# A two-layer encoder trunk: the weight sums' transfers get a list of their own

## The chip, the cores and the metric

The kernel runs on one core of one Trainium2 chip. The metric is device time in microseconds (us): 1640.66 us before the change, the median of three runs from 1640.5 to 1641.07. The engines are TensorE (PE, matrix products), VectorE (DVE), ScalarE (ACT), GpSimd (POOL) and SyncE (SP). SP and POOL also issue DMA transfers, each in the order in which they stand in its own instruction queue; SP's go by DMA queue q1, POOL's by q0.

## The reference

Two layers (DEPTH = 2) over 512 tokens of width 1024, all in float32. Each layer computes

```python
h = _rmsnorm(x, g_mix[l])
proj = h @ w_in[l]                 # 4 gates | conv | three attentions' q, k, v
ys = stack([y_a, y_b, y_c, y_d])   # conformer convolution, neighbourhood, dilated, windowed attention
branch = einsum('bsnc,ncd->bsnd', ys, w_branch[l])
gates = sigmoid(gate_pre + gate_b[l])
x = x + sum(gates * branch, axis=2) @ w_out[l]
x = x + _conv_ffn(_rmsnorm(x, g_ffn[l]), w_up[l], ffn_conv_w[l], ffn_conv_b[l], w_down[l])
```

The feed-forward part (FFN) goes up from 1024 to 2 x 2816, through a width-3 convolution and SwiGLU, and down again to 1024.

## The kernel before

**Products and weights.** Every float32 product is made of three matmuls (lines 273 to 275): both operands are split into a high and a low part. A unit of weights is 512 KB: `weights` (line 248) loads it into a `w_raw` tile, ACT makes `w_hi` (line 252) and DVE `w_lo` (line 254). The units stand in a fixed list, SP issues their loads in that order, and a load waits until its `w_raw` tile is free, that is until the split of an earlier unit is done. There are two `w_raw` tiles; in the FFN two more (`w_more`) are used as well for the units of the "seven" steps, below.

**A layer's stages.** Input projections and attention run interleaved; then come four gates, one after the other (`gates`, line 840), the output projection, and the FFN (`ffn`, line 1052, then `down`). A gate has eight blocks of 24 matmuls. For each block DVE takes the product out of PSUM (`t`, line 849), ACT makes the sigmoid's tanh, and after a short product with the branch's output DVE makes another `t` (line 878) and POOL adds it to the running mix (`mx`, line 879). In the last gate ACT and DVE then split the mix for the output projection (`mh`, line 883, and `ml`, line 884).

**Sums of weights.** Parts of the FFN use products on sums of weight blocks, with seven products in place of eight. The sums are made by DMA in DRAM, all issued by POOL and all behind a matmul that was last when they were written into the program (`paced`). `quarter_sums` makes `qS` for five pieces of the up-projection in 40 transfers of 512 KB. `weight_sums` (line 1133) makes `sums` for the down-projection in 24 transfers: three chunks (1024, 1024 and 768 KB of source) in eight rounds. Rounds 1 and 2 copy a block of W into s3 and s1, rounds 3 and 4 add another block of W to these, round 5 copies s3 to s2, round 6 adds to s2, round 7 copies s2 to s4 and round 8 adds to s4. Copies of s3 and s2 stand in the profile as `sums<-sums`, all else as `sums<-W`. `down` reads `sums`; nothing before it does.

**Side work.** While PE's main stream is written, `tick` (line 887) is called twice a block or unit: in the middle and at the end. Each tick advances every generator in the list `side` by one step: attention, convolution, norms, and the sums, which `slowly` spaces: 12 ticks of delay, then one tick for each quarter sum and four for each weight sum. At the end of the third gate stands

```python
for n in ORDER[:3]:
    self.gates(n)
while self.side:
    self.tick()
```

so that whatever is still in `side` is written into the program there, ahead of the last gate. By then 8 of the 24 weight sums have been written, and the other 16 follow in one run, all behind the same matmul. The output projection has no ticks. The FFN's up-projection begins with 8 ordinary blocks (`whole`), then come 35 "seven" units of 24 shorter matmuls (128x256, line 992) and then 16 ordinary blocks.

Of the kernel before, what the change touches and what calls it, by code (L numbers as in the profile page):

```python
# [218 lines left out]
class Trunk:  # L219
# [667 lines left out]
    def tick(self):  # L887

        for g in list(self.side):

            with self.tc.issue_after(self.last_mm.ins):
                r = next(g, 'end')
            if r == 'end':
                self.side.remove(g)
            if r in ('end', 'free') and g is self.head:
                self.head = None
                self.activate()
        return bool(self.side)

    def activate(self):  # L900
# [422 lines left out]
    def run(self):  # L1323
        nc, tc = self.nc, self.tc
        with ExitStack() as st:
# [36 lines left out]
            self.w_emitted = self.w_used = 0  # L1362
            self.first_hi = None
            self.w_ready, self.w_fast = [], 0
            self.side, self.waiting, self.head = [], [], None

            self.cst = self.const.tile([P, NRES], F32, name="cst", tag="cst", bufs=1)
            self.ident = self.cst[:, C_ID:C_ID + P]
# [40 lines left out]
    def layer(self, l):  # L1409
        tc = self.tc  # L1410
        last = l == L - 1
        self.Y, self.mixed, self.MH, self.glu_u = [None] * 4, [], [], []
        with tc.tile_pool(name="gate", bufs=1, reuse_waits="tile") as self.gp:
            with tc.tile_pool(name="attn", bufs=1, reuse_waits="tile") as self.ap:
                self.scratch = lambda: self.gp.tile([P, S], F32, name="raw", tag="t1", bufs=2)
                pss = self.token_major(None, self.aux) if l == 0 else self.early
                Q = self.new_Q()
                for b in range(NB):
                    self.evac_q(Q)(b, pss[b])
                with self.first():  # L1420
                    for _ in self.qk_stats(Q, 4, 4, None):
                        pass
                self.derive_params()
                V = self.new_V()
                self.tabs = [None] * 4
                self.queue(chain(self.na_biases(l, 3 if l else 5), self.qk_norm(Q, 4, 4, 0),
                                 self.attention('na', V, 1)))
                self.side.append(self.slowly(chain(self.quarter_sums(l), self.weight_sums(l))))
                Vd = self.new_V()
                self.project_v(V, Vd)  # L1430
                Q = self.project_qk()
                ready = self.beside(self.qk_stats(Q, 4, 4, 0))
                self.queue(chain(ready, self.qk_norm(Q, 4, 4, 2), self.attention('dil', Vd, 2)))
                self.glu()
                self.side.append(self.conv())
                V = self.new_V()
                Q = self.project_swa(V)
                ready = self.beside(self.qk_stats(Q, 4, 2, 2))
                self.queue(chain(ready, self.qk_norm(Q, 4, 2, 4), self.attention('swa', V, 3)))
# [4 lines that stand above are left out]
            with tc.tile_pool(name="outp", bufs=1, reuse_waits="tile") as self.op:  # L1444
                self.gates(ORDER[3])
                self.xnew = self.new_res()
                self.start_norm('g_ffn')
                for d in range(0, KT, 2):

                    cuts = (0, KT - 2, KT) if d == 0 else (0, KT)  # L1450
                    pss, ws = [self.mm(), self.mm()], []
                    for k0, k1 in zip(cuts, cuts[1:]):
                        for e in range(2):
                            if k0 == 0:
                                ws.append(self.unit())
                            hi, lo = ws[e]
                            for k in range(k0, k1):
                                s = slice(k * P, (k + 1) * P)
                                self.prod(pss[e], hi[:, s], lo[:, s], self.MH[k][0], self.MH[k][1], k == 0,
                                          k == KT - 1)  # L1460
                            if k1 == KT:
                                self.update(d + e, pss[e], self.op)
                self.xres = self.xnew
                self.broadcast_norm()
        if last:
            self.resT = self.dram.tile([S, D], F32, name="resT", tag="resT", bufs=1)
        with tc.tile_pool(name="ffn", bufs=1, reuse_waits="tile") as self.fp:
            self.scratch = lambda: self.fp.tile([P, S], F32, name="raw", tag="cy0", bufs=2)
            F = self.ffn(l, last)
            if last:  # L1470
                self.down(F, True)
                return
            self.load_prm(l + 1)
            self.xnew = self.new_res()
            self.sq_tag = "fth"
            self.start_norm('g_mix')
            self.down(F, False)
            self.finish_norm(5, 8, 4)

            self.early = self.token_major(None, self.aux)  # L1480
            self.xres = self.xnew
            self.sq_tag = "sq"
# [45 lines left out]
```

## Time and profile before

| | |
|---|---|
| median of three runs | 1640.66 us |
| the profiled execution's own time | 1639.18 us |
| its span, first to last instruction | 1637.4 us |
| mean granted TensorE clock | 0.971 |
| PE busy | 1541.0 us (94%) |
| DVE, ACT, POOL busy | 1251.0, 895.8, 205.4 us |
| `sums<-W`, 24 of 1024 KB and 12 of 768 KB | 12.3 and 16.8 us to landing (median) |
| `sums<-sums`, 8 and 4 | 17.0 and 11.9 us |

The times in a chain or timeline row are start and length in us from the span's start. A row of windows has the busy time of PE, PEld (weight load), DVE, ACT and POOL with the count of instructions, then the granted clock, the mean busy share of the 16 DMA engines, and GB/s. A "wait" names who waited, on whom, us in all, how often, and the longest.

### The profile page before, as it was taken

How to read it: one execution, taken by the hardware profiler on the slowest of the kernel's cores; microseconds unless marked ns; L12 is line 12 of the kernel's file. 1: busy time of each engine (PE TensorE's matmuls, PEld its weight loads, DVE VectorE, ACT ScalarE, POOL GpSimd, SP SyncE). 2: the span in 40 equal slices, each digit the busy share in tenths (PEclk: the TensorE clock that was granted, in tenths of full speed). 3: DMA queues.
4: the chain of work that ended last, by engine and by line, in shares of the span. 5: the costliest groups of instructions: out<-in, count | busy, mean ns of one | idle time of the engine just before them, and what ended most of it. 6: DMA issues, size and time to landing. Idle time of an engine off the chain costs nothing.

```text
span 1637.4 us, 21918 instructions
## 1 busy us (share of the span) xinstructions
PE 1541.0 (94%) x7842; PEld 1311.0 (80%) x7842; DVE 1251.0 (76%) x2114; ACT 895.8 (55%) x1504; POOL 205.4 (13%) x308
## 2 busy tenths in 40 slices
PE   9999999990999999999999999999809999999999
PEld 7888888870788998888888888888708889988887
DVE  6699988740669999986576899887306699999964
ACT  6778777320446665464457686763204556655643
POOL 0044122122110000000002231122221000000000
PEclk9999999995999999999999999999959999999999
DMA  7788764599673554356567988645996747753565
GB/s 233 226 232 229 205 173 142 157 204 236 155 265 103 180 185 136 96 182 202 184 183 222 249 224 197 171 158 157 199 231 170 264 119 209 208 157 93 173 221 166
DMA packets 124797, 306.84 MB, mean 187 GB/s; under 512 B 28176, under 2 KB 30096, under 8 KB 124688
## 3 DMA queue, kind: packets, MB, share of 16 engines
q1 hardware_dynamic: 93712, 212.10, 40.8%
q0 software_dynamic: 30688, 92.81, 25.3%
q8 instruction: 62, 1.02, 0.2%
q10 hardware_dynamic: 288, 0.52, 0.1%
q14 instruction: 47, 0.39, 0.1%
HBM read 287.56 MB, written 100.67 MB: 237 GB/s over the span
## 4 chain that ended last, share of the span: by engine, by line
PE 83%; DMA 6%; DVE 4%; ACT 3%; issue 3%; POOL 2%; SPq 0%; POOLq 0%; ACTq 0%; DVEq 0%
PE mm L273 15%; PE mm L274 15%; PE mm L275 15%; PE aux L992 11%; DMA sums<-sums 4%; PE aux L1225 2%; PE aux L1223 2%; PE aux L1224 2%; PE mm L502 2%; PE mm L504 2%; PE mm L503 2%; PE mm L1224 2%; PE mm L1225 2%; PE mm L1223 2%; PE mm L992 2%
## 5 line engine op out<-in xcount | busy, mean ns | idle before, releaser
L252 ACT ACTIVATE w_hi<-w_raw 128x1024 fp32r<-128x1024 f32 (+1 forms) x335 | 350.9, 1047 | 382.1 <-PE mm L274 127.1
L254 DVE TENSOR_TENSOR w_lo<-w_raw,w_hi 128x1024 fp32r<-128x1024 f32 (+1 forms) x335 | 407.3, 1217 | 94.5 <-ACT w_hi L252 92.3
L273 PE MATMUL mm<-xh,w_hi 128*128 128x512 f32 x960 | 377.3, 393 | 89.5 <-DVE t L849 89.5
L275 PE MATMUL mm<-xh,w_lo 128*128 128x512 f32 x960 | 376.1, 392 | 0.0
L274 PE MATMUL mm<-xl,w_hi 128*128 128x512 f32 x960 | 375.9, 392 | 0.0
L273 PEld LDWEIGHTS mm<-xh,w_hi 128*128 128x128 f32 x960 | 181.5, 189 | 126.9 <-ACT w_hi L252 90.3
L275 PEld LDWEIGHTS mm<-xh,w_lo 128*128 128x128 f32 x960 | 181.1, 189 | 39.7 <-DVE w_lo L254 1.1
L274 PEld LDWEIGHTS mm<-xl,w_hi 128*128 128x128 f32 x960 | 181.6, 189 | 36.4
L992 PE MATMUL aux<-form,w_hi 128*128 128x256 f32 x640 | 116.1, 283 | 0.0
L884 DVE SCALAR_TENSOR_TENSOR ml<-mx,mh 128x512 fp32r<-128x512 f32 x16 | 11.0, 690 | 124.0 <-ACT mh L883 123.8
L992 PEld LDWEIGHTS aux<-form,w_hi 128*128 128x128 f32 x640 | 100.0, 192 | 0.2
L440 DVE SCALAR_TENSOR_TENSOR cv<-cv,prm 128x512 f32<-128x512 f32 x120 | 93.7, 780 | 0.7
L992 PE MATMUL aux<-form,w_lo 128*128 128x256 f32 x320 | 90.6, 283 | 0.0
L879 POOL TENSOR_TENSOR mx<-mx,t 128x512 f32<-128x512 f32 x44 | 65.2, 1487 | 156.7 <-DVE t L878 141.8
L883 ACT ACTIVATE mh<-mx 128x512 fp32r<-128x512 f32 x16 | 10.0, 627 | 135.4 <-POOL mx L879 130.9
L502 PE MATMUL mm<-w_hi,xh 128*128 128x512 f32 x192 | 76.4, 398 | 0.4 <-DVE V L630 0.4
L1033 ACT ACTIVATE cy<-U,prm 128x512 f32<-128x512 f32 x88 | 68.7, 807 | 12.7 <-DVE U L1070 7.6
L503 PE MATMUL mm<-w_lo,xh 128*128 128x512 f32 x192 | 75.0, 390 | 0.0
L504 PE MATMUL mm<-w_hi,xl 128*128 128x512 f32 x192 | 74.8, 390 | 0.0
L1110 POOL DMA_DIRECT2D qS<-W x60 | 43.6, 727 | 217.9 <-PE aux L780 107.0
L767 ACT ACTIVATE e<-e,rl 128x256 f32<-128x256 f32 (+2 forms) x96 | 57.3, 597 | 22.2 <-DVE rl L766 21.9
L849 DVE TENSOR_TENSOR t<-mm,RB 128x512 f32<-128x512 f32 x64 | 43.8, 684 | 30.3 <-PE mm L275 30.0
(339 smaller groups left out, 3297.8 us busy)
## 6 DMA issues: line engine op xcount, KB each, us to landing
w_raw<-W SPq DMA_DIRECT2D x213, 512.0 KB, 3.8
qS<-W POOLq DMA_DIRECT2D x60, 512.0 KB, 6.5
sums<-W POOLq DMA_DIRECT2D x24, 1024.0 KB, 12.3
w_raw<-qS SPq DMA_DIRECT2D x40, 512.0 KB, 3.7
w_raw<-W SPq DMA_DIRECT2D x66, 256.0 KB, 3.9
w_raw<-sums SPq DMA_DIRECT2D x44, 256.0 KB, 3.8
w_raw<-sums SPq DMA_DIRECT2D x22, 512.0 KB, 4.6
qS<-qS POOLq DMA_DIRECT2D x20, 512.0 KB, 4.9
```

The lines of the kernel that those rows point to most:

```text
L252: w = nc.scalar.activation(hi[:, s], raw[:, s], AF.Copy)
L254: nc.vector.tensor_tensor(lo[:, s], raw[:, s], hi[:, s].bitcast(F32), ALU.subtract)
L273: mm(ps, lhsT=wh, rhs=xh, start=start, stop=False)
L274: mm(ps, lhsT=wh, rhs=xl, start=False, stop=False)
L275: self.last_mm = mm(ps, lhsT=wl, rhs=xh, start=False, stop=stop)
L440: self.after_mm(v.scalar_tensor_tensor(acc, u[:, t:t + S], w(t), acc, ALU.mult, ALU.add))
L502: mm(pss[b], lhsT=self.Xh[k][:, t], rhs=hi[:, s], start=k == 0, stop=False)
L503: mm(pss[b], lhsT=self.Xh[k][:, t], rhs=lo[:, s], start=False, stop=False)
L504: self.last_mm = mm(pss[b], lhsT=self.Xl[k][:, t], rhs=hi[:, s], start=False, stop=k == KT - 1)
L992: self.last_mm = nc.tensor.matmul(o, lhsT=w[:, s], rhs=x, start=start and not (e or j or i), stop=j == 3 and i == 2, skip_group_check=True)
L1033: nc.scalar.activation(y, u[:, 1:513], AF.Identity, scale=w(1), bias=self.par('ffn_conv_b', c))
L1223: mm(ps, lhsT=x[0], rhs=w[0][:, cols], start=start, stop=False, skip_group_check=again)
```

## The change

The weight sums' generator (quarter sums and weight sums together) is no longer put into `side`. It goes into a new list `slow`, which `tick` advances after `side`, by one step a tick as before. The loop `while self.side` no longer sees it, so the generator is not emptied ahead of the last gate; the ticks of the last gate and of the FFN carry on with it. The transfers themselves and their pacing on the last matmul stay.

```diff
@@ tick
             if r in ('end', 'free') and g is self.head:
                 self.head = None
                 self.activate()
+        for g in list(self.slow):
+            if next(g, 'end') == 'end':
+                self.slow.remove(g)
         return bool(self.side)
@@ run
-            self.side, self.waiting, self.head = [], [], None
+            self.side, self.slow, self.waiting, self.head = [], [], [], None
@@ layer
-                self.side.append(self.slowly(chain(self.quarter_sums(l), self.weight_sums(l))))
+                self.slow.append(self.slowly(chain(self.quarter_sums(l), self.weight_sums(l))))
```

The order of PE's and of SP's instructions stays as it was. What moves stands on POOL. First place: POOL, first layer, from the end of the third gate into the last one, before. `mx<-mx,t` is the adding of a block to the mix; t_3908 and t_3957 are the last gate's first two. The sixteen rows from `sums_2683` on are the run that is emptied; the first three and the last two are shown.

```order
L879 TENSOR_TENSOR mx<-mx,t_3756 128x512
L1133 DMA sums_2682<-W 512x512
L879 TENSOR_TENSOR mx<-mx,t_3766 128x512
L1133 DMA sums_2683<-W 384x512
L1133 DMA sums_2681<-W 512x512
L1133 DMA sums_2682<-W 512x512
...
L1133 DMA sums_2682<-W 512x512
L1133 DMA sums_2683<-W 384x512
L879 TENSOR_TENSOR mx<-mx,t_3908 128x512
L879 TENSOR_TENSOR mx<-mx,t_3957 128x512
```

The same place after the change (the three chunks are now called sums_2705, 2706 and 2707, and t_3893 is the last gate's first add):

```order
L879 TENSOR_TENSOR mx<-mx,t_3766 128x512
L1136 DMA sums_2706<-W 512x512
L1136 DMA sums_2707<-W 384x512
L879 TENSOR_TENSOR mx<-mx,t_3893 128x512
L879 TENSOR_TENSOR mx<-mx,t_3942 128x512
L1136 DMA sums_2705<-W 512x512
L879 TENSOR_TENSOR mx<-mx,t_3992 128x512
L879 TENSOR_TENSOR mx<-mx,t_4041 128x512
L1136 DMA sums_2706<-W 512x512
L879 TENSOR_TENSOR mx<-mx,t_4097 128x512
L879 TENSOR_TENSOR mx<-mx,t_4146 128x512
L1136 DMA sums_2707<-W 384x512
```

Of the sixteen, four now stand between the last gate's six adds on POOL, and no add stands behind more than two of them. Second place: POOL at the start of the FFN, after the change. `xf<-res` loads the FFN's input for the sums of its own blocks; before the change nothing of `sums` stood there.

```order
L946 DMA xf<-res_4187 128x512
L946 DMA xf<-res_4188 128x512
L1136 DMA sums_2705<-sums_2705 512x512
L1136 DMA sums_2706<-sums_2706 512x512
L1136 DMA sums_2707<-sums_2707 384x512
L1136 DMA sums_2705<-W 512x512
L1136 DMA sums_2706<-W 512x512
L1136 DMA sums_2707<-W 384x512
```

These rounds 5 and 6 and, behind them, rounds 7 and 8 (six more rows) are now written by the ticks of the up-projection, four ticks apart; the second layer is moved in the same way.

## Prediction

> **What bounds the kernel now.** I began with the page's slices: PE is busy nearly everywhere, but for one empty slice in each layer.
>
> ```profile
> PE   9999999990999999999999999999809999999999
> ```
>
> The groups (busy and mean of one, then idle time before it and its releaser) and the list of waits say what ends the empty stretches:
>
> ```profile
> L273 PE MATMUL mm<-xh,w_hi 128*128 128x512 f32 x960 | 377.3, 393 | 89.5 <-DVE t L849 89.5
> L883 ACT ACTIVATE mh<-mx 128x512 fp32r<-128x512 f32 x16 | 10.0, 627 | 135.4 <-POOL mx L879 130.9
> ```
>
> ```profile
> PE mm L273 <- DVE t L849: 89.5, 2, 45.1
> PE aux L1378 <- DVE warm L1375: 1.2, 1, 1.2
> ```
>
> All of PE's idle time worth naming is one wait on `t` (line 849), twice: 45.1 us and, by difference, 44.4. ACT's `mh` in turn waits for POOL's `mx`.
>
> The chain of work shows who holds `t`. These pieces (start, length) are from the first layer's last gate:
>
> ```profile
> 334.87 0.76 POOL mx L879
> ...
> 339.69 3.00 POOL sums L1133 x3
> ...
> 356.62 20.82 DMA sums<-sums
> ...
> 380.29 14.96 DMA sums<-W
> ...
> 395.66 9.81 DMA sums<-sums
> ...
> 408.16 0.95 POOL sums L1133
> 409.11 1.29 POOL mx L879
> 410.42 0.64 ACT mh L883
> ...
> 411.69 0.69 DVE t L849
> ...
> 412.52 0.76 PE mm L273
> ...
> 416.92 0.36 PE mm L273
> 417.28 0.23 PE mm L274
> ```
>
> From 339.69 on POOL issues the run of 16 sums. Rounds 5 to 8 each need the round before to have landed, and POOL waits for that in its queue. The last gate's first add stands behind the run, at 409.11; ACT's `mh` waits for the add, DVE's `ml` for `mh`, and the next block's `t` stands behind `ml` on DVE. PE has run ahead as far as its PSUM banks go and then stops. The windows tell the same: while the 16 DMA engines are full, PE does 1.42 us of work in 46.
>
> ```profile
> 343.00:366.00 23.00, 23.00 (x103) 19.05 (x102) 5.05 (x6) 3.48 (x5) 2.71 (x4) 1.00 1.09 243
> 366.00:412.00 46.00, 1.42 (x7) 0.84 (x5) 0.92 (x2) 1.57 (x2) 9.39 (x11) 0.57 1.03 232
> 520.00:630.00 110.00, 110.00 (x875) 108.07 (x875) 105.02 (x140) 72.79 (x95) 0.00 (x0) 1.00 0.53 173
> 1340.00:1450.00 110.00, 110.00 (x882) 108.40 (x881) 105.83 (x138) 72.53 (x94) 0.00 (x0) 1.00 0.73 201
> ```
>
> So two things are to be weighed: the stall that goes, and what the twelve sums that now run in the FFN do to its weight loads (the last two rows, the seven stages of the two layers, where PE and DVE are both full).
>
> **What goes.** The waits: 89.5 us. Behind each, PE runs at a lower granted clock (0.57 in the stretch that holds the first). From 412.52 to 417.28 ten matmuls start, 4.76 us, where a step at full clock is 0.23 us, as at 417.28: 2.3 us, so 2.5 are lost. In the second layer thirteen start between these two pieces of the chain:
>
> ```profile
> 1227.19 0.77 PE mm L273
> ...
> 1233.14 0.24 PE mm L274
> ```
>
> That is 5.95 us in place of 13 x 0.23 = 3.0, so 3.0 are lost. Together 89.5 + 2.5 + 3.0 = 95.0 us. No other wait of PE is over 1.2 us, and PE's order is the same, so nothing on PE grows behind it.
>
> **What is late next in the last gate.** Four of the sums stand between the six adds on POOL. The third gate shows what that is like:
>
> ```profile
> 322.08 1.06 POOL L1133 DMA_DIRECT2D sums<-W  x1 [6.91 <-PE aux L478]
> 328.81 1.29 POOL L879 TENSOR_TENSOR mx<-mx,t 128x512 f32<-128x512 f32 x1 [4.36 <-DVE t L878]
> ```
>
> A sum takes POOL 1.06 us and is released by PE, and POOL then waits 4.36 us for DVE: POOL is early. Each of the four adds to what has been written many transfers before, so POOL should not wait for a landing. Cost nothing; if they held POOL, that is rival C. The stored sums are not late: twelve of them, four ticks apart, are written by the 48th of the up-projection's 118 ticks, and `down` reads them after that. The quarter sums move past one or two small POOL operations; POOL idles before them, so this costs nothing.
>
> **What the sums cost in the FFN.** Four of the twelve fall on the first eight blocks, 24 matmuls x 0.23 = 5.5 us each, where a unit is wanted only every 5.5 us: nothing. The other eight, 7424 KB (7.6 MB), fall on the seven stage, of which this is a piece of the chain:
>
> ```profile
> 540.06 17.28 PE aux L992 x144
> ```
>
> 144 matmuls, 24 a unit, in 17.28 us: a unit passes in 2.88 us, and eight sums, two units apart, are issued in 46 us. How early the loads are there shows the timeline: a split, the load that it lets go, and that load's own split, four units on (four `w_raw` tiles); below it the loads' median in that stage.
>
> ```profile
> 561.72 1.21 DVE L254 TENSOR_TENSOR w_lo<-w_raw,w_hi 128x1024 fp32r<-128x1024 f32 x1
> 562.96 0.33 SPq L248 DMA_DIRECT2D w_raw<-W  x1
> 571.71 1.06 ACT L252 ACTIVATE w_hi<-w_raw 128x1024 fp32r<-128x1024 f32 x1 [0.69 <-PE aux L992]
> ```
>
> ```profile
> w_raw<-qS SPq DMA_DIRECT2D x18, 512.0 KB, 3.4
> ```
>
> A load thus has 571.71 - 562.96 = 8.75 us; it needs 3.4 there, so 5.3 are spare. Beside sums it needs more: here a lone sum with a load (322 to 323 us), and a load in the full run (343 to 346).
>
> ```profile
> sums<-W POOLq DMA_DIRECT2D x1, 1024.0 KB, 14.5
> w_raw<-W SPq DMA_DIRECT2D x1, 512.0 KB, 8.6
> ```
>
> ```profile
> w_raw<-W SPq DMA_DIRECT2D x1, 512.0 KB, 10.0
> ```
>
> 8.6 to 10.0 us: about 1.3 more than there is, once, if loads that are under way together keep the pace. Whether they do is read from 357 to 362 us, where a pair of loads runs against two or more sums (packets, MB, share of 16 engines); below it the second layer's small stores:
>
> ```profile
> q0 software_dynamic: 263, 0.52, 55.6%
> q1 hardware_dynamic: 250, 0.96, 50.9%
> ```
>
> ```profile
> resT<-xn SPq DMA_DIRECT2D x32, 64.0 KB, 3.8
> ```
>
> q1 moved 0.96 MB in 5 us, 192 GB/s, and q0 104. The first layer's seven stage wants 173 GB/s by its window (0.524 MB in 2.88 us is 182): the loads keep pace, and only the 1.3 us for the first late one are lost; I take 1. The second layer's wants 201, since it stores the residual stream's transpose (`resT`) beside the loads. 7.6 MB at 104 GB/s last 73 us, in which q1 falls 9 GB/s x 73 us = 0.66 MB short, 1.25 units, 3.6 us of PE; I take 3, since part of the 5.3 spare us is left. Bounds: 0 (the spare time swallows it; below nothing is excluded, since PE has no idle time there to win back) and rival A's upper end. I stay near the lower end because the 357 to 362 row has both queues full, which is the state in question.
>
> Sum: 95 - 1 - 3 = 91 us. The profiled execution took 1639.18 (its span of 1637.4 and 1.8 around it) and becomes 1548.2; the median of the runs is 1.5 above it, 1640.66 - 91 = 1549.7.
>
> **Rival A: the sums take the loads' share (0.33).** By time rather than bytes: the run of sums cost
>
> ```profile
> q0 software_dynamic: 3991, 10.69, 102.8%
> ```
>
> 102.8% of 46 us for 10.69 MB, 4.42 us a MB, so eight sums are 33.6 us of all engines. Loads and stores want 0.53 and 0.73 of the engines. If each queue gets half, the sums last 67 us; the second layer falls behind by 0.23 x 67 / 0.73 = 21 us less 5 spare, 16, the first by 0.03 x 67 / 0.53 = 4, nothing after the spare time. With 1 for the first late load: 1640.66 - 95 + 17 = 1563. If the sums always go first, loads get 46 - 33.6 = 12.4 us of 46 where they want 24.4 and 33.6: behind by 12/0.53 - 5 = 17 and 21.2/0.73 - 5 = 24, together 1587. For it: 105 of 110 us busy on DVE, so a late split is not made up. Against it: the 192 GB/s. The Trainium skill ("DMA: Bandwidth & Descriptors", section "Queues, rings and completion order") says that each engine goes round its queues, a whole packet of descriptors from one before the next, whatever their size. By that rule the second layer's stores, cut small, would give a full turn to the sums for few bytes of their own, and the time would go to this rival's upper half; the first layer agrees with near one to one in the row above, 263 and 250, while no row here has small stores beside sums.
>
> **Rival B: slower than before (0.05).** If loads beside a sum land one at a time, as the lone one did, one each 8.6 us, for as long as twelve sums at 14.5 us run (174 us), a layer gets 20 units and six that were ahead; undisturbed, 26 units take 8 x 5.5 + 18 x 2.88 = 96 us. It loses 78 a layer: 1640.66 - 95 + 156 = 1702. It ends on the slower side once loads land over 5.6 us apart for all that time (47.5 us lost a layer). Against it: 0.96 MB in 5 us is one each 2.7 us.
>
> **Rival C: POOL still waits in the last gate (0.05).** If each of its four sums held POOL for one landing (8.6 to 14.5 us), half of each stall would stay: 1640.66 - 47 = 1593. Against it: the order, in which a round stands three transfers or more behind the one that it needs, and the third gate.
>
> **How the numbers follow.** The forecast, 0 to 9 us lost in the FFN, 1545 to 1555, has 0.57. The range goes from 1543 (nothing lost, and 2 for what runs differ) to 1572, which takes in rival A's equal shares; A's upper part, B and C, some 0.18 in all, lie outside. A measurement tells 0.2%, 3.3 us, from no change. Faster by more: 0.57 + 0.33 + 0.05 less a little, 0.94; slower 0.05; same 0.01.
>
> **What would show it.** Right: no wait of PE on line 849 over 2 us; POOL's adds in the last gate 6 us apart; granted clock 1.0 throughout; `sums` spread over the last gate and some 120 us of the FFN. For the forecast, PE in the two seven stages idle for under 5 us in all. Rival A would show waits of PE on `w_hi` or `w_lo` there, most in the second layer, and loads landing in over 9 us; B the same in the first layer's and in the ordinary blocks too; C POOL idle before sums of the last gate, released by DMA. A wait of `down`'s loads on `sums` would make me wrong in another way.

## The result and the profile after

The changed kernel takes 1586.76 us (median of four runs, 1583.33 to 1588.51), beside 1640.58 us for the kernel before, now the median of four runs: a ratio of 0.9673, 95% interval 0.9653 to 0.9694. It is faster by 54 us where 91 were forecast, and outside the range. The profiled execution's span is 1584.3 us, its mean granted clock 0.99.

The slices of the page after, PE and its clock: the two empty slices are gone, and weaker ones stand a little later in each layer.

```profile
PE   9999999999979999999999999999999789999998
PEclk9999999999989999999999999999999899999999
```

PE's waits after (in all, times, longest). Nothing waits on line 849 any more; what is new are 18.9 us on `U`, the first product of the FFN's up-projection, and 8.2 on `sv`, of the seven stage.

```profile
PE mm L273 <- DVE U L1073: 18.9, 2, 10.4
PE aux L995 <- ACT sv L1007: 8.2, 4, 5.7
```

PE runs the same 7842 matmuls in the same order in both kernels, so the start of each can be compared between the two traces; the difference grows or shrinks only where time is lost or won. By stages (us, minus is won):

| | first layer | second layer |
|---|---|---|
| last gate | -47.3 | -47.5 |
| output projection | +1.2 | 0.0 |
| start of the FFN | +10.8 | +12.4 |
| seven stage | +0.5 | +14.8 |

With 0.5 ahead of all this and 1.5 between the layers, the total is -53.1. So 94.8 us went, as the 95.0 of the forecast; 23 came back at a place that the forecast had at nothing, and 15 in the second layer's seven stage, where it had 3.

The last gate on POOL, first layer: two of the sums, each followed by an add that comes when DVE's `t` is there.

```profile
368.09 1.00 POOL L1136 DMA_DIRECT2D sums<-W  x1
372.01 1.29 POOL L879 TENSOR_TENSOR mx<-mx,t 128x512 f32<-128x512 f32 x1 [2.92 <-DVE t L878]
...
378.40 1.03 POOL L1136 DMA_DIRECT2D sums<-W  x1
385.05 1.29 POOL L879 TENSOR_TENSOR mx<-mx,t 128x512 f32<-128x512 f32 x1 [5.62 <-DVE t L878]
```

The windows of the last gate, of the first layer's seven stage and of the second's beginning (PE, PEld, DVE, ACT, POOL, then clock, DMA share, GB/s). PE does 45.32 of 46 us where it did 1.42, and 44.77 of 45 in the first layer's seven stage, but 24.06 of 32 in the second's, at a clock of 0.91:

```profile
366.00:412.00 46.00, 45.32 (x198) 36.67 (x197) 28.55 (x38) 19.61 (x26) 8.38 (x7) 1.00 0.70 176
...
500.00:545.00 45.00, 44.77 (x374) 44.57 (x373) 41.57 (x56) 29.64 (x39) 5.89 (x7) 1.00 1.06 323
...
1281.00:1313.00 32.00, 24.06 (x187) 23.45 (x186) 20.90 (x28) 14.28 (x18) 2.86 (x4) 0.91 1.09 289
```

**The start of the FFN.** POOL in the first layer, from the last gate's last add on:

```profile
393.21 1.30 POOL L879 TENSOR_TENSOR mx<-mx,t 128x512 f32<-128x512 f32 x1 [6.87 <-DVE t L878]
439.27 0.95 POOL L1136 DMA_DIRECT2D sums<-W  x1 [44.76 <-DVE xl L336]
...
440.02 4.30 POOL L946 DMA_DIRECT2D xf<-res  x7
451.68 0.54 POOL L946 DMA_DIRECT2D xf<-res  x1 [7.36 <-DMA sums<-W]
```

The output projection has no ticks, so the next sum (the twelfth, the last of round 4) is written by the first tick of the up-projection and paced on a matmul there. POOL comes to it at 393 and stands before it until 439.27. Behind it in POOL's queue stand the eight loads of `xf`. Before the change they went out one by one during the output projection, as each piece of the result had been stored (first and last):

```profile
450.76 0.62 POOL L943 DMA_DIRECT2D xf<-res  x1 [6.55 <-DMA res<-xn]
...
484.96 0.54 POOL L943 DMA_DIRECT2D xf<-res  x1 [4.53 <-DMA res<-xn]
```

Now they go out in a burst, behind 768 KB that must be read, added and written in the same DMA queue. The chain of work after shows what that delays:

```profile
394.51 44.74 issue
...
440.02 12.71 DMA xf<-res
452.75 1.35 ACT xf L953 x2
454.12 0.43 DVE forms L958
...
466.05 0.61 DVE U L1073
466.80 0.76 PE mm L273
```

The first `xf` lands after 12.71 us. ACT, in order, waits for it to scale it; DVE's `forms` wait for ACT and stand on DVE ahead of the last steps of the norm (lines 308 to 312), whose `RB` the first `U` needs; PE has filled its PSUM banks and stands. None of it needed `xf` so soon: it is the order on four queues that joins them.

**The second layer's seven stage.** A piece of its chain, and SP's queue there:

```profile
1286.80 18.80 DMA w_raw<-qS
...
1305.71 1.06 ACT w_hi L252
...
1309.68 0.49 ACT sv L1007
...
1310.22 4.96 PE aux L995 x24
```

```profile
1289.86 6.50 SPq L248 DMA_DIRECT2D w_raw<-W  x1
...
1298.16 4.83 SPq L248 DMA_DIRECT2D w_raw<-qS  x1
...
1311.30 0.33 SPq L248 DMA_DIRECT2D w_raw<-W  x1
```

A weight load takes 18.8 us to land, more than twice the 8.75 us that it has, and SP stands 6.50 and 4.83 us in the issue of a load that takes 0.33 otherwise. The two DMA queues (packets, MB, share), first in 27 us of the first layer (500 to 527), then of the second (1281 to 1308):

```profile
q0 software_dynamic: 1516, 3.55, 59.8%
q1 hardware_dynamic: 1266, 4.66, 45.5%
```

```profile
q0 software_dynamic: 1795, 4.56, 73.6%
q1 hardware_dynamic: 3007, 3.27, 39.7%
```

Before the change, with nothing of q0 beside it, q1 had this in the same stages (27 us, 527 to 554, and 25 us, 1340 to 1365):

```profile
q1 hardware_dynamic: 1269, 4.66, 53.7%
```

```profile
q1 hardware_dynamic: 4938, 4.70, 69.6%
```

In the first layer q1 still gets 4.66 MB, 173 GB/s, just what the stage wants: 0.5 us are lost. In the second, with the small stores in q1, its share of the engines falls from 69.6 to 39.7%, and it gets 3.27 MB, 121 GB/s, where it wants 188 to 201.

### The profile page after: what moved, and what is told of

It is laid out like the page before. It is cut to its first block, busy times and chain, and to the rows that moved or that the text cites. A ratio compares the mean times of both kernels' runs of the same rounds, so it can differ in the third digit from the quotient of the medians.

```text
span 1584.3 us, 21946 instructions
## 1 busy us (share of the span) xinstructions
PE 1546.5 (98%) x7842; PEld 1315.5 (83%) x7842; DVE 1251.0 (79%) x2114; ACT 896.5 (57%) x1504; POOL 206.0 (13%) x308
## 4 chain that ended last, share of the span: by engine, by line
PE 76%; issue 7%; DMA 7%; DVE 6%; ACT 4%; POOL 0%; ACTq 0%; POOLq 0%; DVEq 0%
PE mm L273 13%; PE mm L274 13%; PE mm L275 13%; PE aux L995 8%; DMA w_raw<-qS 3%; PE aux L1228 3%; PE aux L1227 3%; PE aux L1226 3%; PE mm L502 2%; PE mm L1228 2%; PE mm L1227 2%; PE mm L1226 2%; PE mm L504 2%; PE mm L503 2%; DMA xf<-res 2%
## 5 line engine op out<-in xcount | busy, mean ns | idle before, releaser
L273 PE MATMUL mm<-xh,w_hi 128*128 128x512 f32 x960 | 377.0, 393 | 18.9 <-DVE U L1073 18.9
L995 PE MATMUL aux<-form,w_hi 128*128 128x256 f32 x640 | 120.0, 289 | 9.6 <-ACT sv L1007 8.2
L995 PEld LDWEIGHTS aux<-form,w_hi 128*128 128x128 f32 x640 | 102.6, 197 | 10.8 <-ACT sv L1007 9.0
L1037 DVE SCALAR_TENSOR_TENSOR cy<-U,prm,cy 128x512 f32<-128x512 f32 x88 | 64.3, 748 | 1.7 <-ACT cy L1036 1.7
L1038 DVE SCALAR_TENSOR_TENSOR cy<-U,prm,cy 128x512 f32<-128x512 f32 x88 | 65.0, 746 | 0.3
```

The lines of the kernel that those rows point to most:

```text
L273: mm(ps, lhsT=wh, rhs=xh, start=start, stop=False)
L995: self.last_mm = nc.tensor.matmul(o, lhsT=w[:, s], rhs=x, start=start and not (e or j or i), stop=j == 3 and i == 2, skip_group_check=True)
```

## The experiments

All start from the changed kernel. The table has the median and, by the same comparison of matmuls with the kernel before, what each run lost at the FFN's start and in the seven stage (first / second layer).

| run | median us | FFN's start | seven stage |
|---|---|---|---|
| changed kernel | 1586.76 | 10.8 / 12.4 | 0.5 / 14.8 |
| one earlier | 1564.73 | 0.0 / 0.0 | 0.6 / 14.3 |
| small twelfth | 1574.33 | 2.0 / 7.2 | 2.2 / 16.0 |
| stores moved | 1571.20 | 9.8 / 11.2 | 0.2 / 0.0 |
| both mended | 1551.51 | 0.0 / 0.0 | 0.7 / 0.0 |
| stores in both layers | 1597.29 | 11.5 / 12.9 | 17.0 / 13.5 |
| whole stores | 1599.76 | 12.7 / 10.7 | 16.2 / 13.8 |
| stores by ACT | 1593.91 | 10.8 / 12.9 | 0.5 / 20.9 |
| bytes only | 1592.35 | 10.3 / 11.9 | 7.1 / 14.2 |
| transposes only | 1591.48 | 10.8 / 13.2 | 0.0 / 17.6 |
| bytes and transposes | 1588.02 | 10.9 / 11.4 | 7.2 / 12.1 |
| load unwaited | 1592.34 | 10.6 / 11.7 | 9.0 / 13.4 |
| pieces unwaited | 1604.89 | 11.1 / 13.0 | 21.6 / 13.5 |

Where only the first layer was touched, the second layer's stage varies from 12.1 to 17.6: what a single profile tells of that stage is good to some 3 us.

**Theories.** For the FFN's start, Q: the eight `xf` loads come late because they stand behind the twelfth sum, on POOL and in its DMA queue. Against it R1: the sum's place doesn't count; and Q1, in which its bytes don't. For the second layer's seven stage, T: it is the stores of the stream's transpose beside the sums; R2: the stores don't count.

**One earlier.** At the third gate's end the sums' list is advanced by one tick more. PE's and SP's order stays, and DVE's and ACT's but for one step a layer, which goes back to its place before the change; each sum is paced on a matmul one tick earlier, so that the twelfth is written in the last gate and stands ahead of its last add on POOL, not in the FFN.

```diff
 while self.side:
     self.tick()
+    for g in self.slow:
+        next(g)
```

> Theory Q: in each layer the twelfth weight sum is released only by the first block of the FFN, stands on POOL ahead of the eight xf loads, and its packets lie ahead of theirs in q0; the loads land 10 us late, ACT and DVE wait for them in order, and PE loses 10.8 and 12.4 us at the start of the two FFNs. Here all sums are released one tick earlier, so the twelfth is released by the last gate; nothing else moves on any engine. Q expects xf loads one by one during the output projection, no PE wait on U at the FFN's start, and 23 us less than the changed kernel: 1564. Rival R1 (the FFN's start is slow because sums run beside its loads at all, whatever the order): the sums still run there, so most of the loss stays, 1578 to 1587.

1564.73 us, ratio 0.954 (0.9524 to 0.9556). POOL, the twelfth sum, and the first and last `xf`:

```profile
389.69 0.94 POOL L1136 DMA_DIRECT2D sums<-W  x1
...
405.61 0.62 POOL L946 DMA_DIRECT2D xf<-res  x1 [4.79 <-DMA res<-xn]
...
439.81 0.54 POOL L946 DMA_DIRECT2D xf<-res  x1 [4.86 <-DMA res<-xn]
```

The sum goes out 50 us earlier, the loads go one by one again, and PE's wait on `U` is gone in both layers. Q holds, R1 falls; the second layer's seven stage isn't touched by it.

**Small twelfth.** The twelfth sum stays where it is, but moves 16 of its 384 rows; the other 368 are left out.

```diff
-                add(part(t, d), part(src, s), accum_op=ALU.add)
+                n = slice(0, 16) if d == s1 and t is items[2][1] else slice(None)
+                add(part(t, d)[n], part(src, s)[n], accum_op=ALU.add)
```

> The twelfth sum moves 16 of its 384 rows (352 rows and 16 of the third chunk's s1 are thus not added), with its place on POOL and its release unchanged. Q as stated, with both halves needed (late issue, and 12 us of packets ahead in q0): the eight loads still go out in one burst after 439 us, but the first lands within 5 us in place of 13, so of the 23 us at the two FFN starts 15 to 21 go: 1566 to 1572. Q1, the late issue alone is the cost: less than 6 us go, 1581 or more.

1574.33 us (1571.68 to 1576.99), between the two, 2 above Q's range. PE's waits and the burst on POOL:

```profile
PE mm L273 <- DVE U L1073: 5.9, 2, 4.2
```

```profile
438.14 3.97 POOL L946 DMA_DIRECT2D xf<-res  x7
```

The wait falls from 18.9 to 5.9 us, and the loss at the two FFN starts from 23.2 to 9.2: the bytes ahead of the loads in the queue make some 60% of it, the late burst itself the rest.

**Stores moved.** `turn_res` is called for two tiles each from unit pair 7 on, behind the sums and the seven stage, instead of for one each from pair 0; its load is pinned behind the matmul written last.

```diff
-        if self.last and i % 2 == 1 and i // 2 < KT:
-            self.turn_res(i // 2)
+        if self.last and i % 2 == 1 and i // 2 >= 7:
+            for d in (i - 15, i - 14):
+                self.turn_res(d)
...
-        nc.sync.dma_start(xr, self.xres[d])
+        self.after_mm(nc.sync.dma_start(xr, self.xres[d]))
```

> The second layer's stores of the transposed residual stream (64 KB, in pieces of 128 bytes), with their loads and DVE transposes, are moved behind the seven stage. Theory T: the loss of 14.7 us in the second layer's seven stage comes from these small stores sharing a queue with the weight loads and the engines with the sums. T expects a loss there of 1 or less, as in the first layer (0.5): 1573. Rival R2 (the second layer's seven stage is late because it began with less lead after a longer stall at the FFN's start, 12.4 against 10.8): the loss stays, 1585 to 1588.

1571.2 us, ratio 0.9583 (0.9568 to 0.9597). The second layer's seven stage loses nothing; of the two waits that were new, only the one on `U` is left:

```profile
PE mm L273 <- DVE U L1074: 16.8, 2, 8.6
```

**Stores in both layers.** The first layer, which lost 0.5, does the second's transposes and stores too, into a tile of its own that nobody reads.

```diff
-        if self.last and i % 2 == 1 and i // 2 < KT:
+        if i % 2 == 1 and i // 2 < KT:
...
-        if last:
-            self.resT = self.dram.tile([S, D], F32, name="resT", tag="resT", bufs=1)
+        self.resT = self.dram.tile([S, D], F32, name="resT", tag="resT", bufs=2)
```

> The first layer also does the loads, transposes and small stores of the residual stream that the second does (into a place that nothing reads); more work, nothing left out. T expects the first layer's seven stage to lose what the second's does, 10 to 15 us in place of 0.5: 1597 to 1602. R2 expects no change there: within 4 us of 1587.

1597.29 us (1596.1 to 1598.49): the first layer's seven stage now loses 17.0, a little over T's 10 to 15. T holds from both sides. Both layers also run the same sums and units, so it is this step that sets them apart. The step is loads, transposes and stores together; which of them costs, these two runs don't tell.

**Both mended.** One earlier and stores moved together.

> Both mends at once: sums released one tick earlier, and the second layer's small stores behind its seven stage. If Q and T are two separate losses, their parts add: 1587 less 22 (the run with the earlier release) less 15.6 (the run with the stores moved), 1549; PE idle for under 5 us in both FFNs. If they are one loss counted twice (an earlier start gives the seven stage its lead back), more than 1557.

1551.51 us (1548.74 to 1552.59), ratio 0.946 (0.9432 to 0.9489): the best version, and the two losses add. Its PE slices' clock, and its longest wait of PE:

```profile
PEclk9999999999999999999999999999999999999999
```

```profile
PE mm L273 <- DVE t L849: 1.8, 2, 1.1
```

**What in the stores costs.** `turn_res` loads a tile, transposes it on DVE and stores it in four transfers of 64 KB, cut into pieces of 128 bytes. Seven runs took it apart. In the first, the first layer has load and transposes as above, but one contiguous store of 256 KB a tile:

```diff
+        if not self.last:
+            nc.sync.dma_start(self.resT.rearrange("(e a) c -> e a c", a=P)[d // 2][:, d % 2 * S:d % 2 * S + S], xn)
+            return
```

> The first layer does the second's residual loads and DVE transposes as in the run with stores in both layers, but stores each result in one transfer of 128 pieces of 2 KB in place of four of 512 pieces of 128 bytes: the same bytes, a sixteenth of the pieces. T (the pieces' number) expects the first layer's seven stage to lose under 3 us: 1587 to 1590. R3 (the DVE transposes in a stage where DVE is full, or the bytes): 10 us or more there, as with small pieces, 1597.

1599.76 us (1598.51 to 1601.0): no better than the pieces, so I took the number of pieces to be refuted. That reading was wrong. SP's waits and the chain show that this run loses by another way, which the small stores did not have:

```profile
SPq L1086 <- DVE xn L1083: 20.7, 5, 11.1
```

```profile
503.00 16.94 DMA xr<-res
...
519.96 0.72 DVE xn L1083
...
520.70 0.32 SPq L1086
```

A tile's load lands after 16.94 us beside the sums, DVE's transpose waits for it, SP's store for the transpose, and behind the store stand weight loads.

**Stores by ACT.** The second layer's small stores are issued by ACT, on its own queue.

```diff
-            nc.sync.dma_start(rows[:, :, d * P + 32 * q:d * P + 32 * q + 32],
+            nc.scalar.dma_start(rows[:, :, d * P + 32 * q:d * P + 32 * q + 32],
```

> The second layer's small stores are issued by ACT, on a DMA queue of their own, and not by SP on the weight loads' queue; all else as in the changed kernel. T1 (the pieces hold up the weight loads because they stand in the same queue, each piece giving a turn to the sums): the loss in the second layer's seven stage falls from 14.7 to under 5, 1577 or less. T2 (the pieces load the 16 engines beside the sums, whatever the queue): the loss stays, 1584 to 1590; more than that if ACT waits in its queue for the transposes.

1593.91 us (1590.0 to 1597.83), and the stage loses 20.9. T1's time did not come, but T1 is not refuted, for this run loses by another way. The weight loads' median time to landing was 15.2 us from W and 11.8 from qS in the changed kernel (1281 to 1308); here, at the same place in the stage (1286 to 1313), it is:

```profile
w_raw<-W SPq DMA_DIRECT2D x3, 512.0 KB, 10.2
w_raw<-qS SPq DMA_DIRECT2D x3, 512.0 KB, 8.8
```

The loads land sooner, and between 1285 and 1330 us SP issues each of them in 0.33 us again. It is now ACT that stands, and what waited there:

```profile
1301.51 8.23 ACTq L1086 DMA_DIRECT2D resT<-xn  x1
```

```profile
ACT w_hi L252 <- issue: 5.5, 1, 5.5
```

An issue that takes 0.31 us elsewhere stands 8.23 us, and ACT's splits wait behind it. The chain goes through a store: it lands after 22.90 us, DVE's transpose waits for it (there are two `xn` tiles), and DVE's split stands behind the transpose.

```profile
1297.34 22.90 DMA resT<-xn
...
1320.36 0.09 DVE xn L1083
...
1321.00 1.19 DVE w_lo L254
```

By these rows the loads fare better without the pieces in their queue; how much of the 14.8 us that would save by itself stays open. The Trainium skill ("DMA: Bandwidth & Descriptors", section "Issuing engines are not separate DMA queues") says that issuing on several engines only saves the issuer's time, usually little beside the transfer. The first half agrees with this run's time and not with its loads, 10.2 us for 15.2; the second does not hold here, with 8.23 us of issue beside stores that take some 20 to land.

**Bytes only, transposes only, and both side by side.** The first layer moves the same bytes as two contiguous copies of 256 KB a tile from DRAM to DRAM, pinned behind a matmul and with nobody waiting; or does the eight transposes of a tile that lies ready, without transfers; or both, unlinked.

```diff
+        if not self.last:
+            to = self.resT.rearrange("(e a) c -> e a c", a=P)
+            for c in range(2):
+                self.after_mm(nc.sync.dma_start(to[d // 2][:, c * S:(c + 1) * S], self.xres[d]))
+            return
```

> The changed kernel, 1587, whose first layer in the seven stage also moves, at the places where the second turns its residual stream, the same bytes as two contiguous DRAM-to-DRAM copies of 256 KB a tile; no SBUF, no transposes on VectorE, nobody waits for them. It leaves the output as it is. T2 (the bytes and turns that these transfers take on the DMA engines beside the sums and the loads): the first layer's seven stage, which lost 0.5, loses 8 or more, 1595 or above, as with the pieces (13.6) or the whole stores (16). R3 (the transposes, on a VectorE that is full there): 1587 to 1590. R4 (the in-order wait of VectorE and SyncE: a store behind a transpose behind a late load): 1587 to 1591.

> The changed kernel, 1587, whose first layer in the seven stage also does the second's eight transposes on VectorE, at the same places, of a tile that lies in SBUF already, with no transfer; what they write is not used. T2: within 2 of 1587. R3: the eight transposes alone bring a loss of 8 or more there, 1595 or above. R4: within 4 of 1587, since nothing is late for them to wait for. If this run and the one with the bytes alone are both within 4 of 1587, it is the wait that joins them.

> The two runs before in one: the changed kernel whose first layer does the bytes (two DRAM copies of 256 KB a tile, a loss of 6.6 us in the seven stage above the changed kernel's) and the eight transposes of a tile that lies ready (no loss above the changed kernel's), side by side, none waiting for another. It leaves the output as it is. If only what the DMA engines carry and VectorE's work count, together (T2 with a full VectorE), the loss is that of the whole stores, 13 to 16 us. If the chain of waits between them makes the other half (R4: SyncE and VectorE stand still in order for a load that is late), it stays at 6 to 8, as with the bytes alone.

Bytes only: 1592.35 us, 7.1 lost in the stage, just under the 8 that T2 wanted and above R4's bound. Transposes only: 0.0 lost there; the median, 1591.48 (1589.43 to 1593.53), lies above R4's bound, but by what other stages lost (17.6 in the second layer's), and R3 falls by the stage itself. Side by side: 7.2, so DVE's work adds nothing. The bytes make 7 of the 16.2 that the whole stores lost; what joins the parts makes the rest. q1 in the same 27 us with the bytes only:

```profile
q1 hardware_dynamic: 1448, 4.75, 46.9%
```

It carries hardly more than without the copies, 4.66 MB, so most of the added bytes come out of the loads. This is no fixed ceiling: with the transposes alone q1 carried 5.00 MB in the same stretch.

**Load unwaited, then pieces put back.** The whole stores again, but the transposes read a tile that lies ready, so nobody waits for the late load; then the same with the small stores in place of the whole one.

```diff
-        nc.sync.dma_start(xr, self.xres[d])
+        load = nc.sync.dma_start(xr, self.xres[d])
...
-        nc.vector.transpose(xn, xr)
+        turn = nc.vector.transpose(xn, xr if self.last else self.RB)
+        if not self.last:
+            self.after_mm(load)
+            self.after_mm(turn)
```

> The whole stores, 1600 and a loss of 16 us in the first layer's seven stage, with one wait gone: the transposes read a tile that lies ready, not the one that is being loaded; loads, transposes and the whole stores of 256 KB behind them stay, so the bytes and the store's wait for its transposes stay. The first layer's stored transpose is of other data, and nothing reads it. R4: VectorE and with it SyncE no longer stand behind the late load, the loss falls to 6 to 9 us, 1590 to 1594. T2 (bytes and VectorE's work only): within 3 of the whole stores, a loss of 13 or more, 1597 to 1602.

> The run before (no transpose waits for a load, a loss of 9 us in the first layer's seven stage), with one thing put back: each tile is stored as the second layer does it, in four transfers of 64 KB cut into pieces of 128 bytes, not in one of 256 KB. What is stored in the first layer is of other data, and nothing reads it. P (small pieces hold the queue that issues them: with them one store on ScalarE stood 8.23 us in its issue and one load on SyncE 6.50, where an issue alone is 0.33): the loss is that of the stores in both layers again, 13 or more, 1596 to 1602, and issues of 4 us and more appear on SyncE from 495 to 535 us. If only bytes and the waits on the late load count, it stays at 8 to 10, 1590 to 1594, and issues stay under 1 us.

Without the wait the loss falls from 16.2 to 9.0 (1592.34 us). With the pieces it is 21.6 (1604.89 us, 1603.14 to 1606.65). q1 in 500 to 527, whole and in pieces, and SP's issues with the pieces:

```profile
q1 hardware_dynamic: 1459, 4.81, 48.2%
```

```profile
q1 hardware_dynamic: 3139, 3.80, 42.8%
```

```profile
506.38 6.64 SPq L248 DMA_DIRECT2D w_raw<-W  x1
...
514.47 7.08 SPq L248 DMA_DIRECT2D w_raw<-qS  x1
```

So the small pieces do cost, 12.6 us in this pair: q1 gets 42.8% of the engines for 48.2, moves 3.80 MB in it in place of 4.81, and SP stands in its issues for 6.64 and 7.08 us. P holds, though the time is 3 above its range. With the load waited for, the pieces had lost 17.0, 8 above the 9.0, so the size is known to some 4 us; and since a tile goes in four transfers in place of one, number and size of transfers are not told apart. The whole stores had lost 7.2 by their chain of waits, which hid the cost of the pieces.

## Why the prediction was wrong

- **What goes: right.** 94.8 us for 95.0, waits and low clock together; POOL's adds come when `t` is there (2.92 and 5.62 us of POOL's idle time ahead of the two shown), and rival C did not come.
- **The step that failed: the count of the sums, and with it a term put at nothing.** The prediction has four of the moved sums in the last gate, cost nothing, and twelve in the FFN, and of these: "Four of the twelve fall on the first eight blocks, 24 matmuls x 0.23 = 5.5 us each, where a unit is wanted only every 5.5 us: nothing." The start of the FFN cost 23.2 us. By the program's own order seven of the 24 sums, not eight, are written before `side` is emptied; so seventeen move, four of them (the eighth to the eleventh) into the last gate and thirteen into the FFN. The twelfth is the last row of the second piece of order in the section on the change: it stands behind all six adds, and I counted it among those between them. Then I asked what the sums in the FFN do to the weight loads, and not what stands behind them on POOL: the third piece of order shows the last two of eight `xf` loads, and the twelfth sum stands ahead of the first. Between its tick and the one before it lies the whole output projection, 45 us in which POOL stands. One tick earlier takes all 23 away; taking 368 of the sum's 384 rows away, 14 of them.
- **The seven stage of the first layer: right,** 0.5 us for 1. q1 got 173 GB/s, and 173 to 182 were wanted.
- **That of the second: wrong in size,** 14.8 for 3. The 192 GB/s came from 5 us with no small stores in them; over 27 us q1 got 173 in the first layer. By my own working that is 28 GB/s short for the 58 us that 7.6 MB take at q0's 3.55 MB in 27 us, 1.6 MB or 3.1 units, 9 us; with the 185 GB/s that q1 got beside the transposes alone it is 5. The 7.1 that the bytes alone cost lie between. The rest is the small pieces: that they take q1's share for few bytes I had named beside rival A and not priced, and that they hold SP in its issues I had not thought of. It was shown in the first layer, where it is 8 to 12.6 us; in the second, its part is only argued, from the 6.50 us issues, from the loads that landed sooner when ACT's queue had the stores, and from 14.8 less 7.1. No run took it alone out of the second layer.
- **Rival A** gave 16 us there by equal shares and 4, nearly all covered, in the first layer; measured are 14.8 and 0.5. Its size, its place and in the main its reason were nearer than the forecast's: the sums took q1's share of the engines, down to 39.7% in the second layer and 45.5% in the first. It named the pieces, which carry fewer bytes in that share, but had no term for them. The rule of the Trainium skill ("DMA: Bandwidth & Descriptors", section "Queues, rings and completion order") that I set beside it, a whole packet from one queue and then from the next, agrees in its consequence: with pieces q1 moved 3.80 MB for 4.81. Whether the turns are one for one is not shown, for the profile counts every piece of 128 bytes as a packet: 3139 of q1 to 1709 of q0, against 1459 to 1480 with whole stores.
- **1563 by rival A's equal shares, with the 23 us that no rival had, is 1586,** near the time measured; that it is so near is in part chance, for it has 17 us where 15.3 were lost and leaves out the 3 of the smaller places. That rival A's upper end, 1587, is the time measured is chance altogether: it has 17 and 24 us in the two seven stages and nothing at the FFN's start. Mended at both places the kernel takes 1551.51, beside the forecast of 1549.7: the forecast priced what the change could bring, not what this version of it meets.
- **Rival B:** in no ordinary block did PE wait for a weight load; one load each 8.6 us did not come.

## What to carry to other kernels

A transfer that is moved later in a program is priced by what now stands behind it in its issuer's queue and in its DMA queue, and by the stretch between two of its ticks in which the queue stands still, not only by the bandwidth that it takes. Read the order ahead of every load that a later stage starts with. Where a queue has just the bandwidth that a stage needs, transfers put beside it cost time (7.1 us for 4 MB here), small pieces more, and moving them to a stage with room (15.6 us won) was worth more than issuing them on another engine (7 lost). And count the moved transfers in the order itself: one of seventeen, at the edge of a stage, was more than half of the error.

## What the runs showed of the hardware

- Loads issued behind an accumulating transfer of 768 KB in POOL's queue landed after 12.8 us (median of eight, 256 KB each), 6.2 behind one of 32 KB, and 3.7 where they went out one by one.
- Beside running sums, over 27 us of the first layer's seven stage, q1 got 45 to 49% of the engines and 4.38 to 5.00 MB without small pieces (six runs), and 41 to 43% and 3.58 to 3.80 MB with them (two runs).
- The issue of a transfer can itself stand: 6.50 us on SP and 8.23 on ACT beside small pieces, where 0.33 and 0.31 are usual. It was the issuer whose queue held the pieces that stood: with the stores on ACT, SP issued its loads in 0.33 again (1285 to 1330 us). The list of waits names no releaser for such time (ACT's split behind it has `issue`); it shows as length of the issue in the engine's queue.
